# Three plain inner tiles, LayerNorm sums on VectorE, paired inverses and paired heads in a two-layer encoder

## The chip, the cores and the metric

The kernel runs on one core of a Trainium2 chip. The metric is the time of one execution on the device, in microseconds; 2104.63 us is the median of three runs before the change (2103.97 to 2108.74). All data are float32. Large products are made from float32 numbers split into a high and a low part (type `float32r`), three TensorE matmuls for one product; small products inside the mixers are plain float32 and take two records each in the profile.

## The reference

Width 1024, 512 tokens, two layers. Each layer is a half-step SwiGLU FFN (inner width 2816), a mixer, a second half-step FFN and a gated embedding, with a LayerNorm after each of the first three.

```python
def reference(x, p, ...):
    for i in range(2):
        x = layer_norm(DN_ALPHA * x + 0.5 * swiglu(x, ffn1_wg[i], ffn1_wu[i], ffn1_wd[i]), ln_g[i, 0], ln_b[i, 0])
        y = mixer_ab(x, ...) if i == 0 else mixer_c(x, ...)
        x = layer_norm(DN_ALPHA * x + y, ln_g[i, 1], ln_b[i, 1])
        x = layer_norm(DN_ALPHA * x + 0.5 * swiglu(x, ffn2_wg[i], ffn2_wu[i], ffn2_wd[i]), ln_g[i, 2], ln_b[i, 2])
        x = x + jax.nn.sigmoid(x @ ple_wg[i] + ple_bg[i]) * (p[i] @ ple_wp[i])
    return x
```

Mixer AB (layer 0) projects x to queries (8 heads of 64), keys and values (2 heads of 64) and two inputs of a recurrence. Each query block of 64 tokens sees its own and two earlier blocks; scores get a distance bias, the softmax has a learned extra term (the sink). The other half of the width runs a short convolution and a gated linear recurrence over time. Mixer C (layer 1) is a gated delta rule with 8 heads of 128: for each head and chunk of tokens it forms a lower triangular matrix N of products of the (normalized) keys with decays, applies the inverse of I + N, and carries a 128 x 128 state from chunk to chunk.

```python
    q = q * lax.rsqrt(jnp.sum(q * q, -1, keepdims=True) + NORM_EPS)
    k = k * lax.rsqrt(jnp.sum(k * k, -1, keepdims=True) + NORM_EPS)
    lmat = jnp.where(strict, jnp.einsum('nbhid,nbhjd->nbhij', kb, k) * decay, 0.0)   # kb = k * beta
    amat = lmat + jnp.eye(CHUNK)
    u = triangular_solve(amat, v * beta); w = triangular_solve(amat, kb * exp(gc))
    # per chunk: v_new = u - w state; o = qg state + attn v_new; state = state * glast + kdec^T v_new
```

## The kernel before, in words

Activations lie in SBUF with features on the partitions: x is eight tiles of 128 x 512 (`xf`), each also split into a high and a low half (`xh`, `xl`). Weights stream from HBM in raw tiles of up to 512 KB, six alive at a time (`fetch`, lines 351 to 357; NRAW, line 38), and are split by ScalarE (the high part) and VectorE (the low part) in `splitter`. All intermediate tiles come from one pool of 87 tiles of 128 x 512 (NBIG, line 1500).

An FFN (`ffn`, line 605) has 22 inner tiles, each needing a gate and an up product. The first NPLAIN = 2 are plain: `group` runs over the eight x tiles and adds 3 matmuls of each weight tile (in the second FFN of a layer in two halves of 256 columns, so that the first half can begin before x is complete). Each other inner tile is a `block` (line 470): the two weight tiles and two token halves are combined so that seven products of half width replace eight, in the order a11, s3, s2, a22, s1, a12, s4. That needs sums of weight tiles (made by VectorE and by accumulating DMA loads issued from GpSimd) and differences of x tiles, made once per FFN by `xforms` and `diffs` (lines 615 and 533). `xforms` then multiplies the two x tiles by ALPHA for the residual (lines 624 to 626). The down products follow in two parts of 11 inner tiles.

LayerNorm: after the last products, `take` (lines 714 and 782) adds each output tile to the residual, squares it on ScalarE and adds tile and square to running sums `s` and `q`; for the tiles before the last two (after an FFN) or last three (after a mixer) these additions are on GpSimd, for the last ones, in token halves, on VectorE. `tail` (line 829) turns the sums of one half into mean and scale by matmuls with a matrix of ones, and `apply` (line 858) normalizes tile by tile and splits x. The embedding's products `ple_p` (5 tiles) stand between a mixer's LayerNorm and the second FFN as cover.

Attention (`attn`, line 1025) is one generator per query head: scores for two query blocks (two matmuls on 64 rows), bias, row maximum, exponential with row sum, four or three transposes, a product with the values into 64 columns, and a multiplication by the reciprocal of the sum; when both heads of a query tile are done, four more transposes bring the output to feature layout.

The delta rule (`gdn`, line 1230) is one generator per head, at most NACT = 3 at a time. It transposes k, v and the normalized k; the row sums of k squared come from ScalarE's accumulation, those of q squared from matmuls with a column of ones; then N, its inverse by doubling (ten groups of 32 x 32 matmuls, then one of transposes and two of matmuls of 64 x 64), then the recurrence over four chunks. The decay rows of a head are broadcast from HBM by a DMA issued when the generator begins.

What is issued when is decided while the program is built. Each engine gets its instructions in one fixed order. TensorE's large matmuls drive the order; after each, `tick` (line 291) lets the generators (sorted by a priority) issue what a cost model (`Eng.cost`) says is due by then. A load is taken to land a fixed 3.5 us after it is issued (line 356). An instruction that has to wait on the chip holds up all that stands behind it on its engine.

Of the kernel before, what the change touches and what calls it, by code (L numbers as in the profile page):

```python
# [42 lines left out]
NPLAIN = 2  # L43
# [174 lines left out]
class Kern:  # L218
    def __init__(self, tc, a, order):
        self.tc, self.nc, self.a, self.order = tc, tc.nc, a, order  # L220
        self.ready, self.avail = {}, {}
        self.V, self.S = Eng(tc.nc.vector, "V", self), Eng(tc.nc.scalar, "S", self)
        self.G, self.PE = Eng(tc.nc.gpsimd, "G", self), Eng(tc.nc.tensor, "PE", self)
        self.cnt = 0
        self.nslot = self.slot = self.pos = 0
        self.st = Stream()
# [378 lines left out]
    def ffn(self, i, n, l):  # L605
# [9 lines left out]
        def xforms(kp):  # L615
# [48 lines left out]
        def part(m, p_):  # L664
            while len(scaled) < KD // 2:
                yield None
# [26 lines left out]
    def ffn_ln(self, i, l, desc, y, nk):  # L693
# [35 lines left out]
        for m in range(KD - 2):  # L729
# [3 lines left out]
            self.spawn(first(p_) if m == 0 else take(m, p_, FULL, True, self.G), 1)  # L733
# [21 lines left out]
    def resid_ln(self, i, l, fac, desc, y, nk, ngroup, nhalf):  # L755
# [45 lines left out]
        for m, p_ in enumerate(ps):  # L801
            self.spawn(first(p_) if m == 0 else take(m, p_, FULL, True, G), 1)
        for m in range(max(ngroup, 1), KD - nhalf):
            self.ahead = AHEADO
            self.spawn(take(m, self.mtile(desc(m), y, nk), FULL, True, G), 1)
# [162 lines left out]
    def mixer_ab(self):  # L968
# [8 lines left out]
        self.on, self.done = {}, {}  # L977
# [5 lines left out]
        def evac(m, p_):  # L983
# [13 lines left out]
            elif kind == "q":  # L997
                self.on[j] = self.tl()
                self.done[j] = 0
                for hh in range(2):  # L1000
                    self.spawn(self.attn(j, hh, t))
                while self.done[j] < 2:
                    yield None
                p_ = yield from self.bank()
                yield self.transposes(p_, self.on[j])
                self.ys[j] = yield from self.split(p_)
                self.psfree(self.V)
# [6 lines left out]
        first = (("k", 0), ("v", 0), ("q", 0), ("bx", 0))  # L1014
# [10 lines left out]
    def attn(self, j, hh, q):  # L1025

        S, V, PE = self.S.l, self.V.l, self.PE.l
        h = 4 * hh + j
        rows = slice(64 * hh, 64 * hh + 64)
        on = self.on[j]  # L1030
        sink = self.col("a_sinks", h)
        while self.kt is None:
            yield None
        kt = self.kt
        for pair in range(2):
            segs = [(0, 0, 128, 0), (1, 0, 256, 128)] if pair == 0 else [(2, 128, 384, 0), (3, 256, 512, 256)]
            n = 384 if pair == 0 else 512
            ps = yield from self.bank()
            yield [PE.matmul(ps[:, c0:c0 + k1 - k0], q[rows, b * P:(b + 1) * P], kt[rows, k0:k1], start=True, stop=True)
                   for b, k0, k1, c0 in segs]  # L1040
            sc = self.tl()
            bias = self.bias[h]
            two = lambda t: t.rearrange("p (b k) -> p b k", b=2)
            if pair == 0:
                yield V.scalar_tensor_tensor(sc[:, 0:n], ps[:, 0:n], 0.125, bias[:, 0:n], ALU.mult, ALU.add)
            else:
                yield V.scalar_tensor_tensor(two(sc), two(ps), 0.125, bias[:, None, 128:384].to_broadcast([P, 2, 256]),
                                             ALU.mult, ALU.add)
            self.psfree(self.V)
            nm, rs, es, rd = (self.tiny(2) for _ in range(4))  # L1050
            if pair == 0:
                for bi, (b, k0, k1, c0) in enumerate(segs):
                    yield V.tensor_reduce(nm[:, bi:bi + 1], sc[:, c0:c0 + k1 - k0], AX.X, ALU.max)
            else:
                yield V.tensor_reduce(nm, two(sc), AX.X, ALU.max)
            yield V.tensor_scalar(nm, nm, sink, -1.0, ALU.max, ALU.mult)
            for bi, (b, k0, k1, c0) in enumerate(segs):
                yield S.activation(sc[:, c0:c0 + k1 - k0], sc[:, c0:c0 + k1 - k0], AF.Exp, bias=nm[:, bi:bi + 1],
                                   accum_out=rs[:, bi:bi + 1])
            yield S.activation(es, nm, AF.Exp, bias=sink)  # L1060
            yield V.tensor_tensor(rd, rs, es, ALU.add)
            yield V.reciprocal(rd, rd)
            pt = yield from self.bank()
            yield self.transposes(pt, sc, n // P)
            ptn = self.tl()
            yield S.copy(ptn[:, 0:n], pt[:, 0:n])
            self.psfree(self.S)
            while self.vtok is None:
                yield None
            po = yield from self.bank()  # L1070
            ops = []
            for bi, (b, k0, k1, c0) in enumerate(segs):
                nk = (k1 - k0) // P
                for kb in range(nk):
                    kblk = k0 // P + kb
                    ops.append(PE.matmul(po[:, bi * 64:bi * 64 + 64], ptn[:, c0 + kb * P:c0 + (kb + 1) * P],
                                         self.vtok[:, kblk * P + 64 * hh:kblk * P + 64 * hh + 64],
                                         start=kb == 0, stop=kb == nk - 1))
            yield ops
            dst = on.rearrange("p (b f) -> p b f", b=4)[:, 2 * pair:2 * pair + 2, rows]  # L1080
            yield V.tensor_tensor(dst, po[:, 0:128].rearrange("p (b f) -> p b f", b=2),
                                  rd[:, :, None].to_broadcast([P, 2, 64]), ALU.mult)
            self.psfree(self.V)
        self.done[j] += 1
# [69 lines left out]
    def mixer_c(self):  # L1154
# [24 lines left out]
        self.spawn(self.ba_proj())  # L1179
        for h in range(8):  # L1180
            self.spawn(self.gdn(h))
        for m, p_ in zip(first, self.group([din(m) for m in first], self.x, halves=True)):
# [47 lines left out]
    def gdn(self, h):  # L1230
        S, V, G, PE = self.S.l, self.V.l, self.G.l, self.PE.l
        blk = lambda t, c: t[:, c * P:(c + 1) * P]
        b3 = lambda t: t.rearrange("p (c j) -> p c j", c=NB)
        hc = lambda t, c: t[:, c * 8 + h:c * 8 + h + 1]
        bc = lambda t: t.rearrange("p (c h) -> p c h", c=NB)[:, :, h:h + 1].to_broadcast([P, NB, P])
# [12 lines left out]
        q2 = self.tl()  # L1248
        yield S.activation(q2, q, AF.Square)
        for c in range(NB):  # L1250
            yield S.activation(blk(junk, c), blk(pk, c), AF.Square, accum_out=ss[:, c:c + 1])
        pw = yield from self.bank()
        yield [PE.matmul(pw[:, c:c + 1], blk(q2, c), self.ones[:, 0:1], start=True, stop=True) for c in range(NB)]
        yield V.tensor_scalar(ss[:, 4:8], pw[:, 0:4], NORM_EPS, None, ALU.add)
        self.psfree(self.V)
        yield V.tensor_scalar(ss[:, 0:4], ss[:, 0:4], NORM_EPS, None, ALU.add)
        yield G.tensor_tensor(rr, ss, self.mhalf, ALU.pow)
# [3 lines left out]
        yield S.copy(vtok, pv)  # L1261
        self.psfree(self.S)
# [377 lines left out]
```

## Time and profile before

| | |
|---|---|
| median of three runs | 2104.63 us |
| the profiled execution | 2109.72 us, span 2107.9 us, mean granted TensorE clock 0.986 |
| busy of the span: TensorE matmul, weight load | 2048.0 us (97%), 1855.7 us (88%) |
| VectorE, ScalarE, GpSimd | 1476.6 us (70%), 1136.3 us (54%), 342.8 us (16%) |
| HBM read | 253.27 MB, mean 121 GB/s |

A TensorE that counts as busy is not at its peak: matmuls overlap, and their price is read from how many start in a stretch. The order of the stretches in the span is: FFN 1 of layer 0 from the start, mixer AB from about 372 us, its output and LayerNorm to 558, FFN 2, the embedding, FFN 1 of layer 1 from about 941, mixer C from about 1316, its output and LayerNorm from 1631 to 1695, FFN 2 and the embedding to the end.

### The profile page before, as it was taken

The page shows a single profiled execution, that of the slowest core. Times are in us where ns is not written, and L with a number is a line of the kernel's source. Part 1 is how long each engine was busy: PE and PEld are TensorE (multiplying, and loading weights), DVE is VectorE, ACT ScalarE, POOL GpSimd, SP SyncE. Part 2 cuts the span into 40 slices and gives each one's busy share as a digit, 9 for nine tenths or more (in the row PEclk, how much of TensorE's full clock was granted, in tenths as well). Part 3 has the DMA queues.
Part 4 walks back from the last instruction along what each step waited for, and adds up shares of the span by engine and source line. Part 5 has one row for each costly group of instructions (what it writes and reads, how often), then busy time and mean ns, then how long its engine had stood idle before and what let it go on. Part 6 is the DMA issues. An engine that isn't in the chain of part 4 may idle for free. (4 is left out here: it accounts for less than half of the span.)

```text
span 2107.9 us, 37477 instructions
## 1 busy us (share of the span) xinstructions
PE 2048.0 (97%) x14653; PEld 1855.7 (88%) x14653; DVE 1476.6 (70%) x2916; ACT 1136.3 (54%) x2507; POOL 342.8 (16%) x352
## 2 busy tenths in 40 slices
PE   6999999999889999999999999999999889999999
PEld 5998998878889899898998998877777789989988
DVE  6754767778887367688754767777776797547676
ACT  5642654666566256465643654664644366436544
POOL 1201213000211022201201213011110202012130
PEclk9999999999999999999999999999999999999999
DMA  6855864112367478424855864132221328558631
GB/s 200 181 154 120 181 165 160 41 49 95 86 133 176 116 159 177 148 66 118 185 142 122 186 148 131 42 85 51 57 60 56 99 54 187 146 125 182 159 108 41
DMA packets 90641, 257.81 MB, mean 122 GB/s; under 512 B 10192, under 2 KB 11360, under 8 KB 90464
## 3 DMA queue, kind: packets, MB, share of 16 engines
q1 hardware_dynamic: 54720, 188.81, 28.5%
q0 software_dynamic: 35744, 66.62, 20.5%
q8 instruction: 115, 1.88, 0.4%
q14 instruction: 62, 0.51, 0.1%
HBM read 253.27 MB, written 2.11 MB: 121 GB/s over the span
## 5 line engine op out<-in xcount | busy, mean ns | idle before, releaser
L157 PE MATMUL ps<-t,t 128*128 128x256 f32 (+3 forms) x13520 | 2004.0, 310 | 36.4 <-ACT t L157 21.3
L157 PEld LDWEIGHTS ps<-t,t 128*128 128x128 f32 (+1 forms) x13520 | 1790.7, 188 | 204.3 <-DVE t L157 28.1
L157 DVE TENSOR_TENSOR t<-wr,t 128x512 fp32r<-128x512 f32 (+1 forms) x697 | 499.6, 743 | 33.5 <-ACT t L157 26.0
L157 DVE TENSOR_TENSOR t<-t,t 128x512 fp32r<-128x512 f32 (+3 forms) x650 | 371.3, 593 | 94.4 <-ACT t L157 81.7
L157 ACT CAST t<-t 128x512 fp32r<-128x512 f32 (+1 forms) x557 | 295.3, 549 | 255.6 <-DVE t L157 243.9
L157 ACT CAST t<-wr 128x512 fp32r<-128x512 f32 (+1 forms) x697 | 395.7, 616 | 35.8 <-PE ps L157 31.8
L157 ACT COPY t<-ps 128x256 f32<-128x256 f32 (+2 forms) x379 | 152.0, 402 | 283.0 <-PE ps L157 282.2
L157 DVE SCALAR_TENSOR_TENSOR t<-ps,t 128x512 f32<-128x512 f32 (+2 forms) x110 | 66.6, 610 | 208.6 <-PE ps L157 208.6
L425 POOL DMA_DIRECT2D wr<-w x80 | 68.9, 862 | 841.0 <-DVE t L157 678.7
L157 ACT ACTIVATE t<-t 128x256 f32<-128x256 f32 (+1 forms) x202 | 100.5, 503 | 193.0 <-DVE t L157 189.9
L425 POOL DMA_DIRECT2D t<-w x160 | 139.0, 988 | 178.2 <-DVE t L157 102.8
L157 DVE SCALAR_TENSOR_TENSOR t<-t,t 128x512 f32<-128x512 f32 (+2 forms) x176 | 106.9, 610 | 78.5 <-ACT t L157 77.2
L157 POOL TENSOR_TENSOR t<-t,t 128x512 f32<-128x512 f32 x56 | 88.3, 1611 | 378.8 <-DVE t L157 378.8
L157 DVE TENSOR_TENSOR t<-t 128x256 f32<-128x256 f32 x192 | 80.6, 422 | 74.9 <-ACT t L157 70.1
L157 ACT ACTIVATE t<-ps 128x256 f32<-128x256 f32 (+2 forms) x172 | 61.4, 362 | 90.3 <-PE ps L157 89.4
L157 DVE TENSOR_TENSOR t<-ps,t 128x256 f32<-128x256 f32 (+2 forms) x196 | 85.2, 434 | 19.1 <-PE ps L157 14.9
L157 DVE SCALAR_TENSOR_TENSOR t<-ps,vec,t 128x511 f32<-128x511 f32 (+3 forms) x92 | 68.4, 746 | 23.6 <-ACT t L157 16.1
L157 DVE TENSOR_TENSOR t<-wr,wr 128x512 f32<-128x512 f32 x80 | 54.8, 685 | 14.5 <-DMA wr<-w 14.5
L157 ACT ACTIVATE t<-t,vec,der 128x256 f32<-128x256 f32 x96 | 55.3, 596 | 5.5 <-DVE t L157 5.5
L157 ACT ACT_TABLE_LOAD x39 | 50.0, 1283 | 9.2 <-DVE t L157 7.6
L157 POOL TENSOR_TENSOR y<-y,sm 128x8 f32<-128x8 f32 (+1 forms) x16 | 23.1, 1443 | 191.4 <-DVE y L157 191.4
L157 PEld LDWEIGHTS ps<-cst,t 128*128 128x128 f32 (+1 forms) x300 | 35.8, 149 | 13.2 <-DVE t L157 3.6
(69 smaller groups left out, 527.5 us busy)
## 6 DMA issues: line engine op xcount, KB each, us to landing
wr<-w SPq DMA_DIRECT2D x344, 512.0 KB, 4.2
t<-w POOLq DMA_DIRECT2D x160, 256.0 KB, 5.9
wr<-w POOLq DMA_DIRECT2D x80, 256.0 KB, 4.6
t<-x SPq DMA_DIRECT2D x8, 256.0 KB, 6.7
t<-p SPq DMA_DIRECT2D x8, 256.0 KB, 4.4
t<-gcd POOLq DMA_DIRECT2D x8, 256.0 KB, 5.3
out<-t SPq DMA_DIRECT2D x7, 256.0 KB, 2.0
t<-bias POOLq DMA_DIRECT2D x8, 192.0 KB, 5.3
```

What stands on the lines that cost most here:

```text
L157: getattr(self.e, op.name)(*op.a, **op.kw)
L425: self.nc.gpsimd.dma_start(t, src, accum_op=ALU.add)
```

## The change

It changes seven things.

- NPLAIN is 3: three plain inner tiles instead of two, 19 blocks per FFN instead of 20. The third is a group of its own at full width.
- The multiplication of x by ALPHA is a generator of its own with low priority.
- The sums of LayerNorm are all on VectorE.
- A load's landing is planned from a running sum over the queue of loads.
- In attention one generator serves the two heads of a query tile. The matmuls of the two heads alternate. The probabilities are scaled by the reciprocal before the transposes (on ScalarE), and the second product gives the output in feature layout, one head in output rows 0 to 63, the other in 64 to 127, so that the last transposes go. The first four projections are k, v and two query tiles.
- The inverse is a generator of its own for two heads, with both heads' small matrices side by side.
- In the delta rule the row sums of q also come from a transpose and ScalarE's accumulation; keys are not normalized in advance but through factors per row (`br`, `nk`), which takes away the transposes of the normalized keys; the scaled copies `kdec` and `vtok` are made by VectorE out of PSUM; NACT is 4.

The instructions on the way, cut to their core:

```diff
-NPLAIN = 2
+NPLAIN = 3
@@ fetch
-            self.landing(t, 3.5)
+            self.dt = max(self.dt, self.PE.t + 1.9) + 0.0057 * src.shape[1] / 4 + 0.1
+            self.landing(t, self.dt - self.PE.t)
@@ ffn
             for m in (k0, k1):
-                yield V.tensor_scalar(xf[m], xf[m], ALPHA, None, ALU.mult)
-            scaled.append(kp)
+                self.spawn(scale(m), 6)
+        def scale(m):
+            yield V.tensor_scalar(xf[m], xf[m], ALPHA, None, ALU.mult)
+            scaled.append(m)
...
-        ps = self.group(descs, self.x, halves=n == 2)
-        for j in range(NPLAIN):
-            self.spawn(evac(j, ps[2 * j], ps[2 * j + 1]), 1)
+        for j0, j1 in ((0, 2), (2, NPLAIN)):
+            ps = self.group(descs[2 * j0:2 * j1], self.x, halves=n == 2 and j0 == 0)
+            for j in range(j0, j1):
+                self.spawn(evac(j, ps[2 * j - 2 * j0], ps[2 * j - 2 * j0 + 1]), 1)
@@ ffn_ln (and twice the same in resid_ln)
-            self.spawn(first(p_) if m == 0 else take(m, p_, FULL, True, self.G), 1)
+            self.spawn(first(p_) if m == 0 else take(m, p_, FULL, True, self.V), 1)
@@ mixer_ab
-        first = (("k", 0), ("v", 0), ("q", 0), ("bx", 0))
+        first = (("k", 0), ("v", 0), ("q", 0), ("q", 1))
@@ attn, for both heads of a query tile
+            yield [PE.matmul(ps[hh][:, c0:c0 + k1 - k0], q[rows[hh], b * P:(b + 1) * P], kt[rows[hh], k0:k1],
+                             start=True, stop=True) for b, k0, k1, c0 in segs for hh in heads]
...
+            for hh in heads:
+                for bi, (b, k0, k1, c0) in enumerate(segs):
+                    yield S.activation(sc[hh][:, c0:c0 + k1 - k0], sc[hh][:, c0:c0 + k1 - k0], AF.Copy,
+                                       scale=rd[:, 2 * hh + bi:2 * hh + bi + 1])
+                pt = yield from self.bank()
+                yield self.transposes(pt, sc[hh], n // P)
...
+        use = ((0, 0, 0, 2, 0), (1, 0, 2, 1, 1), (1, 1, 0, 1, 2), (2, 1, 1, 2, 2), (3, 1, 3, 1, 3))
+        yield [PE.matmul(po[rows[hh], b * P:(b + nb) * P], self.vtok[:, kb * P + 64 * hh:kb * P + 64 * hh + 64],
+                         pts[pair, hh][:, c * P:(c + nb) * P], start=n == 0, stop=n == len(use) - 1, skip_group_check=True)
+               for n, (kb, pair, c, nb, b) in enumerate(use) for hh in heads]
@@ mixer_c
             self.spawn(self.gdn(h))
+            if h % 2:
+                self.spawn(self.inverse((h - 1, h)))
@@ gdn
-        q2 = self.tl()
-        yield S.activation(q2, q, AF.Square)
+        pq = yield from self.bank()
+        yield self.transposes(pq, q)
+        for t, o in ((pk, 0), (pq, 4)):
+            for c in range(NB):
+                yield S.activation(blk(junk, c), blk(t, c), AF.Square, accum_out=ss[:, o + c:o + c + 1])
...
-        yield [PE.matmul(pw[:, c:c + 1], blk(q2, c), self.ones[:, 0:1], start=True, stop=True) for c in range(NB)]
-        yield V.tensor_tensor(b3(ktok), b3(pk), rr[:, 0:4, None].to_broadcast([P, NB, P]), ALU.mult)
-        yield self.transposes(pn, ktok)
-        yield S.copy(kn, pn)
-        yield G.tensor_tensor(b3(kdec), b3(ktok), bc(self.kdf), ALU.mult)
+        yield V.tensor_tensor(b3(kdec), b3(pk), bc(self.kdf), ALU.mult)
-        yield S.copy(vtok, pv)
+        yield V.tensor_tensor(b3(vtok), b3(pv), nk[:, :, None].to_broadcast([P, NB, P]), ALU.mult)
...
+        self.Ns[h] = N
+        while h not in self.Uf:
+            yield None
+        Uf = self.Uf.pop(h)
@@ inverse(hs), new: the old steps at twice the width, one of its four levels
+        while any(h not in self.Ns for h in hs):
+            yield None
...
+            yield V.transpose(gs(Uh, LEVELS[n]), thi)
+            yield [PE.matmul(pw[r, cc], nh[r, cc], tlo[r, c2], start=True, stop=True) for r, c2, cc in minis]
+            yield V.tensor_tensor(p3(Yh), p3(pw[:, 0:H]), lev(n)[:, None, :].to_broadcast([P, nc_ // 2, 32]), ALU.mult)
+            yield [PE.matmul(pw[r, H + cc.start:H + cc.stop], Uh[r, cc], Yh[r, cc], start=True, stop=True)
+                   for r, c2, cc in minis]
+            yield V.tensor_tensor(tlo, tlo, gs(pw[:, H:W], LEVELS[n]), ALU.subtract)
...
-NACT = 3
+NACT = 4
-AB_ORDER = (("bx", 1), ("q", 1), ("g", 0), ("bx", 2), ("q", 2), ("g", 1), ("bx", 3), ("q", 3), ("g", 2),
+AB_ORDER = (("bx", 0), ("q", 2), ("bx", 1), ("q", 3), ("g", 0), ("bx", 2), ("g", 1), ("bx", 3), ("g", 2),
```

Here `minis` runs over four row strips of 32 and, for each, over pairs of chunks (four chunks before, eight now).

## Rows read from the trace of the kernel before

**Rows 1.** Windows: stretch, us; busy (instructions) per engine; clock, DMA share, GB/s.
```profile
200.00:250.00 50.00, 50.00 (x419) 50.00 (x418) 35.46 (x63) 30.50 (x69) 11.45 (x14) 1.00 0.83 172
945.00:980.00 35.00, 35.00 (x156) 28.97 (x156) 32.86 (x66) 19.68 (x39) 4.35 (x5) 1.00 0.36 85
```
**Rows 2.** Waits of TensorE: engine, tile; total us, times, longest.
```profile
PE ps L157 <- ACT t L157: 33.4, 7, 7.2
PE ps L157 <- DVE t L157: 22.4, 16, 10.8
```
**Rows 3.** Windows, one stretch of low clock.
```profile
587.30:594.10 6.80, 3.89 (x17) 3.83 (x18) 6.76 (x21) 2.71 (x7) 0.00 (x0) 0.50 0.00 0
```
**Rows 4.** Timeline of the start: start, duration, instruction, [idle before].
```profile
4.37 11.77 PE L157 MATMUL ps<-t,t 128*128 128x512 f32 x38 [4.37 <-ACT t L157]
19.72 0.69 DVE L157 TENSOR_TENSOR t<-wr,wr 128x512 f32<-128x512 f32 x1 [7.78 <-DMA wr<-w]
26.97 18.19 PE L157 MATMUL ps<-t,t 128*128 128x512 f32 x82 [10.83 <-DVE t L157]
```
**Rows 5.** Timeline of TensorE and window, first blocks of two FFNs.
```profile
590.21 15.04 PE L157 MATMUL ps<-t,t 128*128 128x256 f32 x108 [7.16 <-ACT t L157]
576.00:590.20 14.20, 7.05 (x59) 6.85 (x58) 14.05 (x38) 9.49 (x21) 0.00 (x0) 0.90 0.00 0
989.52 10.74 PE L157 MATMUL ps<-t,t 128*128 128x256 f32 x75 [2.22 <-ACT t L157]
```
**Rows 6.** Timeline of TensorE, LayerNorm after mixer AB.
```profile
541.58 0.58 PE L157 MATMUL ps<-t,o 128*128 128x256 f32 x1 [5.95 <-ACT t L157]
544.04 0.58 PE L157 MATMUL ps<-t,o 128*128 128x256 f32 x1 [1.88 <-DVE t L157]
```
**Rows 7.** Instructions by form, VectorE, 522 to 547 us: busy us, mean ns.
```profile
L157 DVE TENSOR_TENSOR t<-wr,t 128x512 fp32r<-128x512 f32 x9 | 8.8, 982 | 0.0
L157 DVE TENSOR_TENSOR t<-t,t 128x256 f32<-128x256 f32 x8 | 7.2, 915 | 2.6 <-POOL t L157 2.5
L157 DVE TENSOR_TENSOR t<-wr,wr 128x512 f32<-128x512 f32 x2 | 1.4, 682 | 0.0
L157 DVE TENSOR_TENSOR t<-t,t 128x256 fp32r<-128x256 f32 x2 | 0.8, 412 | 0.0
```
**Rows 8.** Window of the same LayerNorm; timeline of VectorE, the first splits of x.
```profile
522.00:558.00 36.00, 28.16 (x183) 26.44 (x182) 31.19 (x56) 18.30 (x39) 14.87 (x12) 0.86 0.37 89
552.88 1.10 DVE L157 TENSOR_TENSOR t<-t,t 128x256 fp32r<-128x256 f32 x3 [0.94 <-ACT t L157]
```
**Rows 9.** Window of mixer AB; its large matmuls by form.
```profile
394.00:512.00 118.00, 118.00 (x597) 93.02 (x596) 90.98 (x199) 76.23 (x179) 0.00 (x0) 1.00 0.20 63
L157 PE MATMUL ps<-t,t 128*128 128x512 f32 x344 | 92.1, 405 | 0.0
```
**Rows 10.** Timeline of TensorE in mixer C; window; large matmuls by form.
```profile
1425.88 0.33 PE L157 MATMUL ps<-t 32*32 32x32 f32 x16
1426.13 0.73 PE L157 MATMUL ps<-t,t 128*128 128x512 f32 x2
1426.79 0.33 PE L157 MATMUL ps<-t 32*32 32x32 f32 x16
...
1446.63 1.40 PE L157 MATMUL ps<-t,t 128*128 128x512 f32 x5
1447.87 0.95 PE L157 MATMUL ps<-cst,t 128*128 128x1 f32 x8
1448.67 1.07 PE L157 MATMUL ps<-t,t 128*128 128x512 f32 x4
...
1376.00:1640.00 264.00, 261.59 (x2607) 202.28 (x2607) 189.47 (x508) 139.25 (x384) 39.14 (x37) 0.99 0.23 61
L157 PE MATMUL ps<-t,t 128*128 128x512 f32 x599 | 210.7, 442 | 0.0
```
**Rows 11.** Timeline of VectorE, first head of mixer C.
```profile
1373.24 0.69 DVE L157 TENSOR_TENSOR t<-t,cst 128x512 f32<-128x512 f32 x1 [4.25 <-DMA t<-gcd]
```

More of the change, by code (lines that the diff above doesn't have):

```diff
@@ L664, in part @@
         def part(m, p_):
-            while len(scaled) < KD // 2:
+            while len(scaled) < KD:
                 yield None
@@ L997, in evac @@
             elif kind == "q":
[L998 to L1007, printed above, removed]
+                self.spawn(self.attn(j, t))
             else:
@@ L1023, in mixer_ab, with attn @@
         self.resid_ln(0, 1, 1.0, lambda m: (lambda k: ("ab_out", 0, k, m)), self.y, KD, 4, 3)
-    def attn(self, j, hh, q):
+    def attn(self, j, q):
         S, V, PE = self.S.l, self.V.l, self.PE.l
[L1028 to L1031, printed above, removed]
+        heads = range(2)
+        rows = [slice(64 * hh, 64 * hh + 64) for hh in heads]
+        hs = [4 * hh + j for hh in heads]
+        sink = [self.col("a_sinks", h) for h in hs]
+        two = lambda t: t.rearrange("p (b k) -> p b k", b=2)
         while self.kt is None:
@@ L1037, in attn @@
             n = 384 if pair == 0 else 512
[L1038 to L1048, printed above, removed]
@@ L1061, in attn @@
             yield V.tensor_tensor(rd, rs, es, ALU.add)
             yield V.reciprocal(rd, rd)
[L1063 to L1078, printed above, removed]
@@ L1086, in conv @@
+        self.ys[j] = yield from self.split(po)
+        self.psfree(self.V)
     def conv(self, p_, cols, bias=None):
@@ L1291, in gdn @@
-        yield V.tensor_tensor(c3(U), c3(U), self.icomp[:, None, :].to_broadcast([P, NB, 32]), ALU.add)
-        yield V.transpose(Tt, U)
-        Uf, at = self.tl(), self.tl()
-        yield G.memset(Uf, 0.0)
-        pA = yield from self.bank()
-        yield [PE.matmul(blk(pA, c), blk(kn, c), blk(q, c), start=True, stop=True) for c in range(NB)]
-        pw = yield from self.bank()
-        def lohi(t, s):
-            v = t.rearrange("p (b g two s) -> p b g two s", two=2, s=s, g=16 // s)
-            return v[:, :, :, 0, :], v[:, :, :, 1, :]
@@ L1322, in gdn @@
-        yield V.transpose(U, Tt)
-        self.psfree(self.V)
-        qg = egb
-        Uf3 = b3(Uf)
-        pairs = [(c, slice(o, o + 32), slice(o + 32, o + 64), slice(32 * c, 32 * c + 32)) for c in range(NB) for o in (0, 64)]
-        pw = yield from self.bank()
-        yield [PE.matmul(pw[g, cc], N3[f, c, g], Tt[f, cc], start=True, stop=True) for c, f, g, cc in pairs]
-        Y = Y2
-        yield [V.tensor_copy(Y[o + 32:o + 64, :], pw[o + 32:o + 64, 0:P]) for o in (0, 64)]
-        yield [S.copy(Uf3[32 * b:32 * b + 32, :, 32 * b:32 * b + 32], c3(U)[32 * b:32 * b + 32]) for b in range(4)]
@@ L1332, in gdn @@
-        yield [PE.matmul(pw[f, cc], Y[g, cc], U[g, cc], start=True, stop=True) for c, f, g, cc in pairs]
-        yield [V.tensor_scalar(Uf3[o:o + 32, :, o + 32:o + 64], c3(pw[o:o + 32, 0:P]), -1.0, None, ALU.mult) for o in (0, 64)]
-        self.psfree(self.V)
-        lo, hi = slice(0, 64), slice(64, 128)
-        pw = yield from self.bank()
-        yield [PE.transpose(pw[lo, 64 * c:64 * c + 64], Uf3[lo, c, lo], self.ident[lo, lo]) for c in range(NB)]
-        TA = self.tl()
-        yield V.tensor_copy(TA[lo, 0:256], pw[lo, 0:256])
@@ L1350, in gdn @@
-        yield V.tensor_scalar(Uf3[lo, :, hi], pw[lo, 0:256].rearrange("p (c j) -> p c j", c=NB), -1.0, None, ALU.mult)
-        self.psfree(self.V)
+        yield V.tensor_tensor(b3(vtok), b3(pv), nk[:, :, None].to_broadcast([P, NB, P]), ALU.mult)
+        self.psfree(self.V)
+        pA = yield from self.bank()
+        yield [PE.matmul(blk(pA, c), blk(k, c), blk(q, c), start=True, stop=True) for c in range(NB)]
+        at = self.tl()
+        yield V.tensor_tensor(at, pA, dt, ALU.mult)
+        self.psfree(self.V)
@@ L1359, in gdn @@
             if c:
-                yield PE.matmul(pw[:, 0:P], blk(kn, c), st, start=True, stop=True)
+                yield PE.matmul(pw[:, 0:P], blk(k, c), st, start=True, stop=True)
                 r = r_
```

202 lines of the change are left out of this document (127 added, 75 removed).

## The prediction

> **What bounds the kernel now.** I read the profile in this order: busy shares, waits by engine, granted clock, then the stretches around each long wait. TensorE is the bound: 97% busy, and its sequence of instructions is fixed. The price list comes first. In a block of seven products nothing waits: 419 matmuls of 256 columns in 50 us, less two cut off at the edges, is 0.120 us each; 512 columns cost 0.227 us (154 in 35 us) [rows 1]. TensorE waits little in sum, 33.4 us for ScalarE results and 22.4 us for VectorE results, but in few pieces [rows 2]. After such a wait its granted clock is at the lower level (0.50, that is 1.2 GHz) for a while, in seven stretches besides the first and last microseconds (one of them stands here), and matmuls there take about twice as long [rows 3]. So the time to be won lies in about seven waits with the slow stretches behind them, and in what the small fp32 matmuls of the two mixers cost TensorE.
>
> **The change, part by part.** All sums are against the profiled execution: 2107.9 us span and 1.8 us around it, 2109.7 us; the median of the three timed runs is 5.1 us lower.
>
> *Start.* VectorE stood 7.8 us before an addition of two weight tiles whose load came only at 19.7 us; the splits of x lay behind it in its queue, and TensorE stopped for 10.8 us after 38 of the 96 matmuls of its two plain tiles [rows 4]. The planner had put every weight load 3.5 us after its issue. The change sums the queue up (13.5 us when the constants are issued, 1.56 us for each 512 KB after that), and with a third plain tile the first six loads feed plain tiles, which need no such addition. Without the wait the 58 matmuls that were left at 15.8 us end at 15.8 + 58 x 0.227 = 29.0 us; in the trace they end at 27.0 + 18.2 us less 24 matmuls of the next block at 0.12, 42.3 us. Of these 13.3 us I count 12, since the x forms of the first block must now be ready earlier. Bounds: 4 (another early load stands in the way) and 14.
>
> *Third plain tile.* A plain inner tile is 48 matmuls of 512 columns, 10.9 us; the block that it replaces is 84 of 256, 10.1 us [rows 1]: 0.8 us dearer, four times. What it buys is cover. At the start of FFN 2 TensorE waits 7.2 us for the x differences (in both layers), at that of FFN 1 in layer 1 2.2 us; VectorE is the late one, 14.05 of 14.2 us busy [rows 5]. The following low clock costs 17 matmuls x (0.229 - 0.120) = 1.9 us [rows 3], by the same working about 1.4 us in layer 1's FFN 1. Scaling x later takes its multiplications out from before the last needed difference, and the third tile puts four weight splits there; I let these cancel within 1 us. TensorE comes there 10.9 us later, which covers the 7.2. Gain: 7.2 + 1.9 - 0.8 = 8.3 us at each FFN 2, 2.2 + 1.4 - 0.8 = 2.8 us at the other.
>
> *LayerNorm sums on VectorE.* After each mixer TensorE waits 5.95 + 1.88 us for the sums [rows 6]. GpSimd makes eight of them by the code, and while it does, VectorE's nine splits take 0.98 us where 0.68 is usual, eight half-width additions 0.92 where 0.41 is for that width; VectorE also waits 2.5 us for GpSimd [rows 7]. Moved to VectorE, eight additions at 0.60 us (start to start) cost 4.8; 9 x 0.30 + 8 x 0.50 = 6.7 us of blocking and 2.5 + 1.0 us of waits go: everything behind comes 5.4 us earlier. TensorE's work in the 36 us stretch [rows 8] is 144 half-width matmuls, 30 full ones and eight sums: 17.3 + 6.8 + 0.9 = 25.0 us, 11 us less than it took. But the next group can start only with x: its first piece was split at 553.3 [rows 8], now at 547.9; TensorE began the group at the end of the stretch, 557.7. So 9.8 us, less 1.4 us because the last x half comes later than the faster group wants it: 8.4 us. After the FFNs no such wait exists; there the ten additions moved count nothing, hidden under TensorE's output tiles (if the cover fails, 10 x 0.60 = 6 us each). Together with FFN 2 16.7 us a layer; I count 33 for both.
>
> *Attention in pairs.* In its 118 us there are 344 large matmuls, 78.1 us; 39.9 us go to small fp32 ones and to the switches between them [rows 9]. A group of small matmuls costs about 0.2 us beyond its own time: from 1425.88 to 1426.79 us lie one group and two large matmuls, 0.91 - 0.45 = 0.46 us, 0.25 of it its own [rows 10]. By the code 53 groups become 29: 24 x 0.2 = 4.8 us; the four transposes of the output go (1.4 us); the second product has twice the columns and fewer instructions (+0.8 us). That is 5.4 us, the lower bound. If both heads, on different rows (scores) or output columns (second product), run side by side, half of their 12 + 12 us (0.1 us for each 128 columns of a record) goes too: 17.4. I take the middle, 11. The 16 records of a 32x32 group start within 0.25 us where records alone need 0.10 each [rows 10], so row strips do overlap here; output strips on the same rows this trace doesn't show. The Trainium skill ("TensorE: Matmul & The Clock Gate", Part 3, Packing small matmuls) says that weight loads overlap running matmuls only where the row group differs; by that the scores overlap and the second product doesn't, and this part gives 5.4 + 6 = 11.4 us. The added ScalarE scalings (32 at 0.4 us) are hidden: ScalarE has 76 of 118 us work.
>
> *Delta rule in pairs.* The 264 us hold 599 large matmuls, 136 us; 128 us go to small ones [rows 10]. An inverse is 13 groups per head, ten of 32x32 and three of 64x64: 104 groups become 52. Removing a 32x32 group saves 0.46 us less what the doubled one adds, 0 to 0.25; halfway 0.34: 40 x 0.34 = 13.6. The twelve others save the switch, 2.5. The row sums of q (five large matmuls and the group from 1446.63 to 1448.67: 0.90 us) go eight times: 7.2. Transposes of q replace those of k. Sum 23.3, bounds 18 and 30. VectorE gains and loses about as much (two wide products added, one removed, half of the inverses' small steps) and keeps slack, 189 of 264 us. I take off 3 us: heads 6 and 7 now end together, with little behind them. So 20.
>
> *Broadcast load.* VectorE waits 4.25 us for the decay rows of the first head, TensorE some 3 us of its 22.4 behind that [rows 2, 11], and the low clock that follows costs about 2 [rows 3]: 5.3 us. That addition now stands behind four more squares, a product and the power: I count 4.
>
> Sum: 12 - 0.8 + 2.8 + 33 + 11 + 20 + 4 = 82 us. 2109.7 - 82 = 2027.7; as a median 5.1 lower: **2022 us**.
>
> **Rivals.** *VectorE takes over.* At the seams it is full [rows 5], and it gets more work there and a faster TensorE behind it. Then each layer's seam gives 7 instead of 16.5, attention 5, the delta rule 12 (waits in its chain), the start 11, the others 4.8: 47 us, 2058. For it: the saturated row; against it: what GpSimd blocked comes back. *Everything comes*: 13.5 + 3.5 + 36 + 17 + 30 + 5 = 105 us, 2000. For it: the strips overlap in 32x32 form. *Slower: buffers run out in the delta rule.* Four heads are active instead of three, and head 2n holds its tiles until 2n+1 has its own matrix; all share 87 tiles with the weight splits. If splits wait for tiles, TensorE starves and falls to 1.2 GHz; were half of the large matmuls there at that level (68 us) with 30 us of waits, the result is 2104.6 - 62 + 98 = 2140. It decides from 62 us on (82 less this part's 20), some 8 us a head. Against it: the stretch has 261.6 of 264 us busy, so three heads come nowhere near it. *The change doesn't do what it says*: loads planned too late keep the start as it is: 2033, inside my range.
>
> **How the numbers follow.** Forecast 0.60 (own range 2006 to 2042), VectorE 0.22, everything 0.10, slower 0.05, no change 0.03. The range of 1997 to 2061 leaves out the slower case, no change and the outer part of the second and third. A measurement can tell about 0.3% (6 us) from no change: faster 0.92, same 0.03, slower 0.05.
>
> **What would show it.** Right: TensorE's waits at about 16, 535, 583, 1673 and 1720 us gone or under 2 us, with no low clock behind them; no GpSimd additions before a LayerNorm and no VectorE instruction of 1.5 us there; no 128x1 matmuls and half as many 32x32 groups, each with 32 records; some 30 us less for the delta rule with its load wait. Wrong: a wait of 5 us or more on VectorE at the first block of an FFN, scores of two heads that start a full matmul apart, or low clock inside the delta rule.

## The result, and the profile after

The changed kernel takes **2032.33 us** (median of four runs, 2032.03 to 2032.67) against 2106.2 us for the kernel before in the same comparison: ratio 0.9649, 95% interval 0.9632 to 0.9666. The forecast was 2022 us, range 1997 to 2061. The profiled execution took 2032.03 us, so it stands for the median.

The page of the changed kernel (engine, busy us and share, instructions), then its waits (engine, tile; total us, times, longest), which answer to [rows 2]:

```profile
span 2030.2 us, 36724 instructions
PE 1999.5 (98%) x14397; PEld 1816.5 (89%) x14397; DVE 1436.7 (71%) x2856; ACT 1127.4 (56%) x2531; POOL 236.2 (12%) x276
```
```profile
PE ps L157 <- ACT t L157: 15.6, 5, 4.7
PE ps L157 <- DVE t L157: 10.8, 18, 2.2
DVE t L157 <- DMA wr<-w: 12.2, 4, 4.1
```

TensorE's waits have halved, from 55.8 to 26.4 us, and the stretches of low clock went from seven to two, not counting the one at the very end of each trace. The two traces are cut at the first and last matmul against the matrix of ones in each LayerNorm; the pieces, in us:

| stretch | before | after | difference | forecast |
|---|---|---|---|---|
| start to the first LayerNorm's sums | 316.1 | 303.2 | -12.9 | -11.2 |
| mixer AB | 143.7 | 131.0 | -12.7 | -11 |
| LayerNorm after the mixer, layers 0 and 1 | 40.8, 40.5 | 27.9, 28.3 | -12.9, -12.2 | -8.4 each |
| second FFN, layers 0 and 1 | 304.5, 305.6 | 308.6, 307.2 | +4.1, +1.6 | -8.3 each |
| embedding and FFN 1 of layer 1 | 341.5 | 338.4 | -3.1 | -2.8 |
| mixer C with its load wait | 338.0 | 308.4 | -29.6 | -24 |

All else agrees within 0.1 us; the sum, -77.7, is the difference of the two profiled executions (the medians differ by 73.9). What failed is the seam between a mixer and the second FFN: 8.8 and 10.6 us instead of 16.7 each.

TensorE at the start (start, duration, instruction, [idle before]) answers to [rows 4]. The wait of 10.8 us is 0.36, and 1.5 us are left before the first block:

```profile
4.13 32.73 PE L157 MATMUL ps<-t,t 128*128 128x512 f32 x132 [4.13 <-ACT t L157]
37.22 7.33 PE L157 MATMUL ps<-t,t 128*128 128x512 f32 x48 [0.36 <-DVE t L157]
46.06 4.22 PE L157 MATMUL ps<-t,t 128*128 128x256 f32 x33 [1.51 <-ACT t L157]
```

TensorE at the second FFN of layer 0 answers to [rows 5, 6]; the waits in the LayerNorm are gone, but two new ones stand among the second halves of the first two plain tiles. Layer 1 has the same two at 1631.5 and 1637.7 (2.18 and 4.69 us).

```profile
518.61 7.76 PE L157 MATMUL ps<-t,t 128*128 128x512 f32 x57
526.73 7.46 PE L157 MATMUL ps<-t,t 128*128 128x256 f32 x60 [0.36 <-DVE t L157]
536.32 1.45 PE L157 MATMUL ps<-t,t 128*128 128x256 f32 x10 [2.13 <-DVE t L157]
542.37 17.81 PE L157 MATMUL ps<-t,t 128*128 128x256 f32 x98 [4.61 <-ACT t L157]
```

VectorE in the same place (timeline), then a piece of the chain of waits (start, us, what):

```profile
530.98 0.69 DVE L157 TENSOR_TENSOR t<-wr,wr 128x512 f32<-128x512 f32 x1
...
533.44 2.49 DVE L157 TENSOR_TENSOR t<-wr,t 128x512 fp32r<-128x512 f32 x4
...
536.18 0.48 DVE L157 SCALAR_TENSOR_TENSOR t<-t,der,t 128x256 f32<-128x256 f32 x1
540.67 0.69 DVE L157 TENSOR_TENSOR t<-wr,wr 128x512 f32<-128x512 f32 x1 [4.01 <-DMA wr<-w]
541.28 0.42 DVE L157 TENSOR_TENSOR t<-t 128x256 f32<-128x256 f32 x1
```
```profile
533.44 0.70 DVE t L157
534.13 0.02 issue
534.15 6.42 DMA wr<-w
```

The first sum of weight tiles (`t<-wr,wr`) is that of the first block, the second that of the second block, needed only after the whole first block. It is early in VectorE's order, its load is issued when the split at 533.4 gives a raw tile back, and VectorE stands still for it. The planner allows such a load 1.9 + 1.56 us when its queue is empty; this one took 6.42. Whether a longer allowance would have moved the sum was not tried. The next piece of x (541.28, `apply`) lies behind it; ScalarE's half of that piece waits for VectorE, so TensorE's wait bears ScalarE's name. It is the fault of the start [rows 4] in another place.

VectorE has no room there to catch up. The window (columns as in [rows 1]):

```profile
518.50:537.00 18.50, 16.01 (x125) 15.31 (x124) 17.56 (x40) 14.90 (x33) 1.75 (x2) 1.00 0.41 108
```

### The profile page after: what moved, and what is told of

Its sections match the earlier page's. It is cut to its first block, busy times and chain, and to the rows that moved or that the text cites. A ratio compares the mean times of both kernels' runs of the same rounds, so it can differ in the third digit from the quotient of the medians.

```text
span 2030.2 us, 36724 instructions
## 1 busy us (share of the span) xinstructions
PE 1999.5 (98%) x14397; PEld 1816.5 (89%) x14397; DVE 1436.7 (71%) x2856; ACT 1127.4 (56%) x2531; POOL 236.2 (12%) x276
## 4 chain that ended last, share of the span: by engine, by line
PE 87%; DVE 7%; ACT 3%; DMA 1%; issue 1%; POOL 0%; SPq 0%; DVEq 0%; ACTq 0%
PE ps L157 87%; DVE t L157 7%; ACT t L157 3%; DMA wr<-w 1%; ACT L157 0%; DVE y L157 0%; POOL y L157 0%; ACT y L157 0%; SPq L1456 0%; DVEq L157 0%; DVE der L157 0%; ACTq L157 0%
## 5 line engine op out<-in xcount | busy, mean ns | idle before, releaser
L157 PE MATMUL ps<-t,t 128*128 128x256 f32 (+4 forms) x13984 | 1973.4, 305 | 26.9 <-ACT t L157 15.6
L157 PEld LDWEIGHTS ps<-t,t 128*128 128x128 f32 (+2 forms) x13984 | 1771.2, 183 | 200.4 <-DVE t L157 26.6
L157 DVE TENSOR_TENSOR t<-wr,t 128x512 fp32r<-128x512 f32 (+1 forms) x697 | 456.6, 682 | 23.3 <-ACT t L157 15.5
L157 DVE TENSOR_TENSOR t<-t,t 128x512 fp32r<-128x512 f32 (+3 forms) x694 | 392.3, 589 | 84.5 <-ACT t L157 76.8
L157 ACT CAST t<-t 128x512 fp32r<-128x512 f32 (+1 forms) x545 | 286.9, 547 | 232.4 <-DVE t L157 230.1
L157 ACT COPY t<-ps 128x256 f32<-128x256 f32 (+2 forms) x347 | 136.6, 396 | 254.3 <-PE ps L157 254.1
L157 ACT ACTIVATE t<-t 128x256 f32<-128x256 f32 (+1 forms) x190 | 94.1, 501 | 191.9 <-DVE t L157 188.6
L157 ACT ACTIVATE t<-ps 128x128 f32<-128x128 f32 (+2 forms) x204 | 70.9, 358 | 94.6 <-PE ps L157 93.6
L157 DVE TENSOR_TENSOR t<-wr,wr 128x512 f32<-128x512 f32 x76 | 52.0, 685 | 12.2 <-DMA wr<-w 12.2
L157 ACT ACT_TABLE_LOAD x39 | 50.0, 1283 | 11.4 <-DVE t L157 8.5
L157 DVE SCALAR_TENSOR_TENSOR t<-t,der,t 128x256 f32<-128x256 f32 x96 | 45.5, 478 | 0.0
L157 DVE TENSOR_TENSOR t<-t,ps 128x512 f32<-128x512 f32 (+1 forms) x62 | 33.4, 579 | 13.9 <-PE ps L157 11.2
```

The costliest lines, as they stand in the source:

```text
L157: getattr(self.e, op.name)(*op.a, **op.kw)
```

## The experiments

The median of the kernel before is 2106.2 to 2108.3 us in the five comparisons, so 1 or 2 us between two runs decide nothing by themselves; there the stretches of the two traces are compared.

**1. The order of the weight sums at the second FFN.**
```diff
         for j0, j1 in ((0, 2), (2, NPLAIN)):
+            self.ahead = 3 if n == 2 and j0 == 0 else 6
```


> The changed kernel, but while the first two plain tiles of a second FFN run, weights are prepared three steps ahead instead of six, so that the sum of the second block's weight tiles comes behind the last pieces of x on VectorE. Theory (queue): VectorE stands 4.0 us before that sum at 540.7 (and the same in layer 1), TensorE waits 4.6 us behind it and then runs at the low clock; both go, 4.6 + 3.2 us in layer 0 and 4.7 + 1.8 us in layer 1: 2032 - 14 = 2018 us, range 2014 to 2024, and TensorE's waits of 4.6 and 4.7 us are gone. Rival (throughput): VectorE is full there whatever the order, 17.6 of 18.5 us; the wait only moves: 2029 to 2035 us with 4 us or more of waits left at each of the two places.

Measured: 2022.04 us (2020.16 to 2022.33), ratio to before 0.9595 (0.9581 to 0.961). The long wait is gone in both layers, the shorter one stayed; TensorE and then VectorE:

```profile
529.51 3.31 PE L157 MATMUL ps<-t,t 128*128 128x256 f32 x22 [0.73 <-DVE t L157]
533.08 0.50 PE L157 MATMUL ps<-t,t 128*128 128x256 f32 x2 [0.26 <-ACT t L157]
535.79 24.42 PE L157 MATMUL ps<-t,t 128*128 128x256 f32 x146 [2.20 <-DVE t L157]
```
```profile
528.43 0.69 DVE L157 TENSOR_TENSOR t<-wr,wr 128x512 f32<-128x512 f32 x1 [0.37 <-DMA wr<-w]
...
532.91 2.49 DVE L157 TENSOR_TENSOR t<-wr,t 128x512 fp32r<-128x512 f32 x4
```
So the queue theory holds for 10 of its 14 us. Before the wait that is left VectorE has four weight splits, its own work. This is the fastest version found.

**2. Two plain tiles**, all else as changed.
```diff
-NPLAIN = 3
+NPLAIN = 2
-        for j0, j1 in ((0, 2), (2, NPLAIN)):
+        for j0, j1 in ((0, 2),):
```


> The changed kernel with two plain inner tiles instead of three. Theory of the prediction (the third tile is cover): TensorE waits again 7 us for the x differences at each second FFN and 2 us at FFN 1 of layer 1, with low clock behind: 2 x 8.3 + 2.8 us more, and at the start the first block's needs come 10.9 us earlier, 0 to 8 us more: 2032 + 19 to 27 = 2051 to 2059 us. Rival (the cover is eaten by the new wait for the second block's weights): the third tile is worth nothing at the second FFNs, 2030 to 2042 us.

Measured: 2066.31 us (2063.01 to 2068.3), 34.0 more than the changed kernel. By stretches: start 5.9, second FFNs 13.0 and 10.4, FFN 1 of layer 1 4.1 us. The third tile is cover, and worth more than forecast. It is worth more where the sums are on VectorE: there the second FFNs take 318.8 and 319.9 us with two plain tiles (experiment 5) and 308.6 and 307.2 with three; with the sums on GpSimd they take 304.5 and 305.6 (the kernel before) and 301.4 and 298.0 (experiment 3; the other parts of the change differ too). At the start, where the new planning stays but the third tile is missing, TensorE waits 5.07 us:

```profile
23.21 15.83 PE L157 MATMUL ps<-t,t 128*128 128x512 f32 x72 [5.07 <-DVE t L157]
```

**3. Sums on GpSimd** (the same in the two calls of `resid_ln`).
```diff
-  take(m, p_, FULL, True, self.V), 1)
+  take(m, p_, FULL, True, self.G), 1)
```


> The changed kernel with the LayerNorm sums of the early output tiles on GpSimd again. Theory of the prediction: 8.4 us more after each mixer, nothing after the FFNs: 2049 us; by the stretches of the two traces (12.9 and 12.2 us shorter) 2057 us; VectorE instructions beside GpSimd's take 0.9 us where 0.4 is usual. Rival: the gain of these stretches comes from the shorter queue before the FFN and not from the engine of the sums: under 2037 us.

Measured: 2033.74 us (2032.07 to 2034.66), 1.4 more, which is noise (the two profiled executions differ by 0.04 us): on the rival's side, but not for its reason. By form, VectorE and GpSimd between 496 and 521 us and then VectorE in the changed kernel between 496 and 514; last TensorE and VectorE with the sums on GpSimd:

```profile
L157 DVE TENSOR_TENSOR t<-wr,t 128x512 fp32r<-128x512 f32 x9 | 12.6, 1421 | 0.0
L157 POOL TENSOR_TENSOR t<-t,t 128x512 f32<-128x512 f32 x8 | 11.5, 1454 | 152.7 <-DVE t L157 151.7 <-DMA wr<-w 1.0
```
```profile
L157 DVE TENSOR_TENSOR t<-wr,t 128x512 fp32r<-128x512 f32 x3 | 2.1, 684 | 0.0
```
```profile
512.62 0.38 PE L157 MATMUL ps<-t,o 128*128 128x256 f32 x1 [4.31 <-ACT t L157]
514.17 0.58 PE L157 MATMUL ps<-t,o 128*128 128x256 f32 x1 [1.17 <-DVE t L157]
```
```profile
543.06 0.69 DVE L157 TENSOR_TENSOR t<-wr,wr 128x512 f32<-128x512 f32 x1 [1.68 <-DMA wr<-w]
```
The splits beside GpSimd's additions take 1421 ns instead of 684, and the LayerNorm stretches are 7.8 and 9.5 us longer, as forecast. But the second FFNs are 7.2 and 9.2 us shorter: when x comes later, the load of the second block has nearly landed (VectorE waits 1.68 us for it). One wait stands in for the other.

**4. Both edits together**: the lines of 1 and 3.

> Both edits together: LayerNorm sums on GpSimd, and weights three steps ahead in the first plain tiles of a second FFN. Theory (one wait for the other): the sums on VectorE do bring x 7.2 and 9.3 us earlier, as between the two traces with and without them; in the changed kernel that is given back in the wait for the second block's weights, which come no earlier. With that wait away the sums must show: 2022 + 16 = 2038 us, range 2033 to 2041, so no faster than with the sums alone on GpSimd (2034) or little. Rival (the engine of the sums is indifferent, something else hides it): 2020 to 2026 us.

Measured: 2029.82 us (2029.0 to 2032.75), 7.8 more than experiment 1; below the theory's range, above the rival's. The sums give 6.3 and 9.4 us in the LayerNorm stretches, of which the second FFNs take back 4.2 and 4.9 (TensorE's 2.2 us wait for VectorE in experiment 1, and the low clock behind it).

**5. The sums alone, on the kernel before** (in all three calls).
```diff
-  take(m, p_, FULL, True, self.G), 1)
+  take(m, p_, FULL, True, self.V), 1)
```


> The kernel before with one part of the change alone: the LayerNorm sums on VectorE. By the prediction's term, 8.4 us less after each mixer and nothing after the FFNs: 2106 - 17 = 2089 us, range 2086 to 2092. Rival (what is won at the sums is given back at once, as VectorE stays full until the first blocks of the FFN): TensorE's wait of 7.2 us there grows by as much, 2100 to 2107 us. Between: half given back, as between the two runs with three steps ahead (7.8 us for both layers), 2098 us.

Measured: 2113.37 us (2110.48 to 2115.61), ratio 1.0026 (1.0016 to 1.0035): slightly slower, beyond the rival. The LayerNorm stretches shrink to 28.4 us each (12.4 and 12.1 won), the second FFNs grow by 14.4 and 14.3. Again VectorE stands before an early sum, and later TensorE waits for the x differences as in [rows 5]:

```profile
557.94 0.69 DVE L157 TENSOR_TENSOR t<-wr,wr 128x512 f32<-128x512 f32 x1 [3.57 <-DMA wr<-w]
```
```profile
559.02 3.78 PE L157 MATMUL ps<-t,t 128*128 128x256 f32 x16 [4.66 <-DVE t L157]
564.98 16.46 PE L157 MATMUL ps<-t,t 128*128 128x256 f32 x114 [2.18 <-DVE t L157]
583.60 0.50 PE L157 MATMUL ps<-t,t 128*128 128x256 f32 x2 [2.15 <-ACT t L157]
...
590.47 1.77 PE L157 MATMUL ps<-t,t 128*128 128x256 f32 x6 [4.27 <-ACT t L157]
```

**6. Two further orders at the seam.** First the edit of 1 with a split ahead of x only when it is needed next; then the edit of 1 with 2 for 3.
```diff
-        prio = 0 if self.nsplit <= self.pos + 2 else 4
+        prio = 0 if self.nsplit <= self.pos + self.urgent else 4   # urgent 0 in the first two plain tiles of a second FFN, else 2
```


> As the edit that prepares weights three steps ahead in the first plain tiles of a second FFN, and there a weight split goes ahead of the pieces of x only when it is needed next (before: two steps ahead). Theory (order on VectorE): the 2.2 us that TensorE still waits at 533 and 1624 us stand behind a burst of four weight splits between two pieces of x; without the burst both waits fall under 1 us: 2022 - 4 = 2018 us, range 2015 to 2020. Rival (throughput): VectorE is full over the whole stretch, the third tile's weights are now late instead, a wait of 2 us or more appears some 10 us later: 2021 to 2026 us.

> Weights two steps ahead, instead of three, in the first two plain tiles of a second FFN. With three steps four weight splits stand in a row between the last pieces of x and TensorE waits 2.2 us at 533 and 1624 us; holding those splits back altogether made the third tile late by 3 to 4 us. With two steps pairs of splits alternate with pieces of x. Theory (the order decides, and there is one that hides both): waits under 1.5 us at both places, 2022 - 3 = 2019 us, range 2016 to 2021. Rival (VectorE's work of the stretch is the bound, an order only moves the wait): 2021 to 2026 us, with 2 us or more of waits in each second FFN.

Measured: 2030.89 us (2030.49 to 2031.19) and 2024.62 us (2024.09 to 2027.02). In the first the waits in the halves fall to 1.1 us (layer 1: 1.5), but the third tile's weights are late, and a weight sum waits 4.19 us for its load at 555.6 with splits of that tile behind it (TensorE, then VectorE). The rival's picture was right, its size too small:

```profile
548.82 10.05 PE L157 MATMUL ps<-t,t 128*128 128x512 f32 x36 [3.13 <-DVE t L157]
562.62 7.61 PE L157 MATMUL ps<-t,t 128*128 128x512 f32 x43 [3.75 <-DVE t L157]
```
```profile
555.59 0.69 DVE L157 TENSOR_TENSOR t<-wr,wr 128x512 f32<-128x512 f32 x1 [4.19 <-DMA wr<-w]
```
In the second the waits in the halves are 1.08 and 1.10 us, as its theory wanted, but 1.39 and 1.06 us (layer 1: 2.50) appear at the first block, and the time is in the rival's range. So of three orders each moved what is left; none removed it.

**7. Loads planned 3.5 us after issue.**
```diff
-            self.landing(t, self.dt - self.PE.t)
+            self.landing(t, 3.5)
```


> The changed kernel with every weight load planned 3.5 us after its issue again; the third plain tile stays. Theory (the planned landing is what ends the wait at the start): VectorE stands before a weight sum again, TensorE waits some 10 us in the first 40 us: 2041 to 2044 us. Rival (the third plain tile does it, since the first six loads need no sum): the start stays as it is, 2029 to 2036 us.

Measured: 2035.11 us (2034.41 to 2036.84), 2.8 more. With six loads that need no sum the third tile removes most of the wait at the start; 1.48 and 2.10 us remain without the plan.

**8. x scaled at once.**
```diff
-                self.spawn(scale(m), 6)
+                yield V.tensor_scalar(xf[m], xf[m], ALPHA, None, ALU.mult)
+                scaled.append(m)
```


> The changed kernel with x multiplied by ALPHA at once after the differences again, ahead of later differences on VectorE. The prediction let this cancel against the splits of the third tile within 1 us at each FFN. Theory: with the third tile as cover the multiplications hide, 2030 to 2036 us. Rival: VectorE is full at the second FFNs, so six multiplications of 0.4 us before the last needed difference cost 2.4 us and low clock behind, at two to four places: 2037 to 2045 us.

Measured: 2039.93 us (2039.2 to 2040.0), 7.6 more: the rival. At the second FFN of layer 0 TensorE waits again after the third tile, with multiplications (`TENSOR_SCALAR`) between the last differences; layer 1 has 2.40 us at 1669:

```profile
569.57 0.75 DVE L157 TENSOR_SCALAR t<-t 128x512 f32<-128x512 f32 x2
570.24 0.42 DVE L157 TENSOR_TENSOR t<-t,t 128x256 fp32r<-128x256 f32 x1
570.57 0.75 DVE L157 TENSOR_SCALAR t<-t 128x512 f32<-128x512 f32 x2
```
```profile
571.71 3.49 PE L157 MATMUL ps<-t,t 128*128 128x256 f32 x27 [2.46 <-DVE t L157]
```

**9. The two heads in turn.**
```diff
-   ... for b, k0, k1, c0 in segs for hh in heads]
+   ... for hh in heads for b, k0, k1, c0 in segs]
-   ... for n, (kb, pair, c, nb, b) in enumerate(use) for hh in heads]
+   ... for hh in heads for n, (kb, pair, c, nb, b) in enumerate(use)]
```


> The changed kernel with the matmuls of the two heads of a query tile in turn (all of one head, then all of the other) instead of alternating, in scores and second product. Theory (the two heads run side by side: in the trace they start 7 ns apart): half of the time is lost, scores 7.7 us and second product about 6.5 us more: 2045 us, range 2040 to 2048. Rival (only scores, on different rows, overlap; output columns on the same rows don't): 2039 us. Rival (nothing overlaps, records only start early): 2030 to 2034 us.

Measured: 2035.58 us (2034.33 to 2036.35), 3.3 more. By time alone that is near the last rival; the records say otherwise. Mixer AB by form (instructions | busy us, mean ns of one | idle), the kernel before, the changed kernel, the heads in turn:

```profile
L157 PE MATMUL ps<-t,t 128*128 128x64 f32 x112 | 14.2, 267 | 0.0
L157 PE MATMUL ps<-t,t 64*128 64x256 f32 x48 | 13.8, 394 | 0.0
```
```profile
L157 PE MATMUL ps<-t,t 64*128 64x256 f32 x48 | 6.9, 394 | 0.0
L157 PE MATMUL ps<-t,t 128*64 128x256 f32 x32 | 5.0, 392 | 0.0
L157 PE MATMUL ps<-t,t 128*64 128x128 f32 x48 | 4.0, 273 | 0.0
```
```profile
L157 PE MATMUL ps<-t,t 128*64 128x256 f32 x32 | 7.6, 392 | 0.0
L157 PE MATMUL ps<-t,t 64*128 64x256 f32 x48 | 7.0, 394 | 0.0
L157 PE MATMUL ps<-t,t 128*64 128x128 f32 x48 | 6.6, 273 | 0.0
```
As many score records cover half the time, 13.8 to 6.9 us: the heads run side by side, with starts 7 ns apart, and they do so also when they come in turn (13 ns apart). The two rows of the second product overlap in time and can't be added up. By the records of the traces each of its four groups, from its first record to the next matmul, takes 1.67 us alternating and 2.59 in turn: in turn the other head starts only with the seventh of the first head's ten records. That is 3.7 us for the four, near the 3.3 of the run (mixer AB itself is 2.5 us longer). So the experiment did not take the overlap away, it took part of it in one of the two products.

**10. One inverse for each head.**
```diff
-            if h % 2:
-                self.spawn(self.inverse((h - 1, h)))
+            self.spawn(self.inverse((h,)))
```


> The changed kernel with one inverse generator for each head, all else of the new delta rule kept. Theory of the prediction: the pairing is worth 13.6 us for the 32x32 groups and 2.5 us for the twelve others: 2032 + 16 = 2048 us; by the price of the groups in the two traces (80 at 0.55 us against 40 at 0.67 or 0.73; 64x64 groups and transposes some 4 us) 2032 + 20 = 2052 us. Rival (the doubled group costs as much as two): within 5 us of 2032. Rival (pairing costs waits in the chains, heads 6 and 7 ending together): under 2044 us.

Measured: 2045.92 us (2045.33 to 2048.16), 13.6 more, nearest to the first theory; mixer C is 14.2 us longer. The pairing shows in the 32x32 matmuls, the changed kernel and then one inverse for each head:

```profile
L157 PE MATMUL ps<-t,t 32*32 32x32 f32 x1280 | 20.1, 193 | 2.1 <-DVE t L157 1.8
```
```profile
L157 PE MATMUL ps<-t,t 32*32 32x32 f32 x1280 | 28.0, 196 | 0.0
```

**11. Three heads active instead of four.**
```diff
-NACT = 4
+NACT = 3
```


> The changed kernel with three heads of the delta rule active at a time instead of four. Theory of the prediction: buffers don't run out, so the fourth head costs nothing; it fills the waits of a pair for each other's matrix: 2032 to 2040 us. Rival (the fourth head's tiles hold up the weight splits): faster than 2029 us.

Measured: 2063.6 us (2062.27 to 2064.22), 31.3 more: outside what either expected, 23.6 us above the theory's range. The end of mixer C, windows with three heads and with four (this the changed kernel):

```profile
1570.00:1620.10 50.10, 35.73 (x151) 26.64 (x150) 21.64 (x52) 10.22 (x29) 2.01 (x2) 0.69 0.13 38
```
```profile
1550.00:1586.90 36.90, 36.49 (x211) 30.75 (x210) 22.41 (x55) 10.26 (x31) 2.02 (x2) 1.00 0.24 72
```
With three, the last pair is late: at the end TensorE has little but its chain of small matmuls left, waits 3.4 us twice and up to 1.5 us elsewhere, and the clock has a mean of 0.69. Mixer C takes 341.1 us, more than the 338.0 before the change. What a fourth head is worth without the pairs was not tried.

## Why the prediction was right, and where not

*The size.* Right within 10.3 us. The sum was 82 for a measured 77.7: 4.3 us. Another 5.1 us is the step from the profiled execution to the median, which the changed kernel does not have: its profile took 2032.03 us. That the sum came so near is in part luck: the two seams are 13.6 us short of the 33 forecast, the other parts 9.3 us over theirs. Of its signs of being right one failed: waits of 4.6 and 4.7 us with low clock behind them are left near two of the places it named.

*Start* (12 forecast, less 0.8): 12.9, right. Either part does most of it alone: 2.8 us go without the plan, 5.9 without the third tile.

*Third plain tile as cover*: right in kind. The 2.2 us wait in layer 1's FFN 1 is gone (-3.1 for -2.8). At the second FFN the x differences are no longer late, but the gain of 8.3 us did not appear, because of the next point. The clause that let scaling and splits cancel within 1 us failed: scaling later is worth 7.6 us, 6.7 of them in the two second FFNs.

*LayerNorm sums on VectorE*: this is the step that failed. That GpSimd blocks VectorE, and what its leaving brings at the sums, was right (7.8 and 9.5 us in experiment 3, and 12.4 and 12.1 on the kernel before, for 9.8 before the deduction); so was that the additions moved behind the FFNs cost nothing (56.3 and 56.7 us in both traces). The other 5.1 and 2.7 us by which the LayerNorm stretches became shorter no run assigns. The mis-sized term is the deduction, "less 1.4 us because the last x half comes later than the faster group wants it": it is 7.2 and 9.2 us. 10.3 us of both layers together is a cause not in the prediction, the second block's sum placed early on VectorE (experiment 1); the rest stays under all three orders tried (experiments 1 and 6). VectorE's load there (17.56 of 18.5 us) is its likely cause, which no run shows. The rival "VectorE takes over" had the place, and its 7 us for each seam was nearer to the 8.8 and 10.6 than the forecast's 16.5; its lower prices elsewhere were wrong.

*Attention* (11, bounds 5.4 and 17.4): 12.7, and about 14.5 for equal work, since eight more matmuls of 512 columns (0.227 us each) lie in this stretch of the changed kernel. Both products overlap, which was the upper bound's condition. By the records, from the first of a group to the next matmul, the scores fill 15.3 us before and 7.7 after, the second product 11.2 and 6.7: 12.1 us, as that bound had it. The other term, 5.4 for fewer groups and transposes, was too large by this account: 2.4 of the 14.5 are left for it. The rule of the Trainium skill on which the prediction leaned ("TensorE: Matmul & The Clock Gate", Part 3, Packing small matmuls: weight loads overlap running matmuls only for another row group) made 11.4 us of it, near the time but not for the measured reason. The trace differs from it: a weight load of one head begins at 407.873 us, 5 ns after the other head's matmul on the same 128 rows (407.868), and the two heads run side by side on different output columns. A table of the same page ("Why this matters for your kernels") does say that outputs in different column groups gain as different rows do, and this trace agrees with that.

*Delta rule* (20, and 4 for the load): 29.6 together. The pairing gave 13.6 us for 16.1 forecast (experiment 10); the products with ones (7.7 us busy before) are gone, for 7.2; TensorE's wait for the decay rows fell from 3.2 us to nothing that shows, VectorE's from 4.25 [rows 11] to 1.18, with no low clock behind. The products before and VectorE's wait after:

```profile
L157 PE MATMUL ps<-cst,t 128*128 128x1 f32 x64 | 7.7, 241 | 0.0
```
```profile
1336.47 0.69 DVE L157 TENSOR_TENSOR t<-t,cst 128x512 f32<-128x512 f32 x1 [1.18 <-DMA t<-gcd]
```
What the prediction had no term for is the fourth active head. The 3 us that it took off for the last pair were not needed with four heads active; with three, mixer C loses more than it gains from the whole change (experiment 11: 32.7 us against 29.6). Of the three terms only the pairing was taken out by a run, the other two are read from rows; some 4 of the 29.6 us belong to none of them.

*The slower rival* (buffers run out) did not come: with fewer heads active the kernel is slower, not faster. "No change" at the start was wrong as well.

## What to carry to other kernels

A wait that goes away hands its time to whatever is next in the same in-order queue; before counting a gain as such, look at what that queue holds next and when its loads land. Two edits that shift the same queue are not additive: the sums alone cost 5 us or were worth nothing, and with more cover and a better order they were worth 8. An instruction that waits for a load should not stand ahead of work that the bottleneck engine needs sooner, however early it could be done.

## What the runs showed of the hardware

- Two streams of small matmuls on different output columns but the same 128 rows run at the same time (20 records in 1.67 us, with starts 7 ns apart), as those on different rows do. Issued one after the other, the second, in all four groups, starts 0.92 us after the first, with the seventh of its ten records, and then ahead of the first's later ones by its start time (408.527 against 408.737 us, told apart by the sizes of the records).
- A 32x32 group of 32 records takes 0.38 us from its first record to the next large matmul, one of 16 records 0.26 (about 0.1 us of either is a switch behind the last record). The large matmul ahead of it takes 0.1 to 0.2 us more than the usual 0.227 until the group starts. "TensorEngine Tiling (Array Packing)" of the Trainium skill (Key Properties) says that a change of the tiling mode drains TensorE; the extra times agree with that.
- While GpSimd adds 128 x 512 tiles (1.45 us each), a VectorE split of that size takes 1.42 us instead of 0.68 (experiment 3).
